# Four value blocks instead of two at the start of a decoder trunk, and a layer norm whose centering is divided between VectorE and GpSimd

## The chip, the cores and the metric

The kernel runs on one core of one Trainium2 chip. The metric is the device time of one execution in microseconds (us). The engines of the core are named as the profile names them: PE is TensorE (PEld its weight loads), DVE is VectorE, ACT is ScalarE, POOL is GpSimd, and SP issues the DMAs.

## The reference, cut to what matters

The computation is a two-layer decoder trunk on one sequence of 256 tokens with model width 2048, all in float32. Layer 0 mixes tokens with RWKV-7, layer 1 with causal differential attention. Each mixer and each gated MLP (conv-GLU) is followed by a layer norm over `ALPHA * x + h`, so there are four norms.

```python
def rwkv7_mix(x, v_first, vres, mu, w_rkv, w0, w1, w2, ...):
    xx = token_shift(x) - x
    xr, xw, xk, xv, xa, xg = (x + xx * mu[i] for i in range(6))
    r = xr @ w_rkv[0]
    k = xk @ w_rkv[1]
    v = xv @ w_rkv[2]
    w = -jax.nn.softplus(-(w0 + jnp.tanh(xw @ w1) @ w2)) - 0.5
    a = jax.nn.sigmoid(a0 + (xa @ a1) @ a2)
    g = jax.nn.sigmoid(xg @ g1) @ g2
    ...

def reference(x, ...):
    for i in range(DEPTH):
        h = rwkv7_mix(x, ...) or diff_attn_mix(x, ...)
        x = layer_norm(ALPHA * x + h, ln_g[i, 0], ln_b[i, 0])
        x = layer_norm(ALPHA * x + conv_glu(x, ...), ln_g[i, 1], ln_b[i, 1])
    return x
```

## The kernel before

**Layout.** Activations are stored transposed: 128 of the 2048 channels on the partitions, 256 tokens along the free dimension, so an activation is `KT` = 16 tiles of 128x256 ("k-tiles"). A weight matrix is read from HBM in blocks of 128 output channels; a block is 16 weight tiles of 128x128.

**Exact products.** Each float32 operand is split into a high part `hi` (a rounded copy, made by ACT) and a low part `lo` (source minus `hi`, made by DVE). A product of a block and one k-tile is hi*hi, hi*lo and lo*hi, which is three passes of 256 columns on PE. `mm3` (lines 222 to 232) issues them either as one matmul of 512 columns and one of 256 into two halves of a PSUM bank (lines 231 and 232), which `total` then adds, or "narrow" as three of 256 columns into one half (lines 227 to 229), after which one copy is enough. Weights come in DMAs of 256 KB (`raw`), and `chunk` makes `hi` (line 216, ACT) and `lo` (line 219, DVE, or GpSimd where `pool` is set). In the first stage such a chunk is four weight tiles wide (128x512).

**The first stage** is in `rwkv`. It computes the values `V` (16 blocks), three small "lora" products (one block each, `in_l`), and the first four blocks of keys and receptances (`products(0)`). That is 23 blocks, or 23 * 16 * 3 = 1104 passes of 256 columns. Every product needs its own mixture of `x` and the shifted `x`, made by `mix(i, ...)`: `xx` is the difference of neighbouring tokens (line 789), `mx` is `xx * mu + x` (line 792, DVE), and `split` writes its high part (line 196, ACT) and its low part (line 197, DVE) into `S0` or `S1`. The program text of the stage is:

1. `lead` feeds the mixture for the values tile by tile and runs the first `lg` = 2 value blocks beside it. `ramp=2` runs the first chunks of both blocks tile by tile in an order of their own (lines 243 to 258).
2. Then `_together` interleaves the loras with the other value blocks, taken in pairs into one PSUM bank (`dense_pair`).
3. Then come the mixture for the keys and `products(0)`.

**The norms.** `ln_stats` sums the channels by matmuls with a constant matrix into the PSUM tile `lnst`, whose halves are the mean and the mean square. ACT copies the mean to SBUF (`ln_dm`, line 428). DVE forms the variance (`ln_v`, line 429), ACT takes Ln and Exp (lines 434 and 435) for 1/sqrt, and DVE improves it by one Newton step (lines 436 to 438). The first value and the result both lie in the second half of `lnst`. `ln_apply` then centers all 16 tiles of `X` on GpSimd (line 450), and DVE and ACT scale and split them. At three of the four norms this runs beside the first six blocks of the next product, whose matmuls use the tiles before they are normalised (`Ahead`, lines 915 to 917). The fourth norm ends the program (`ln_finish`): there four pairs of tiles are centered by DVE, straight from the mean in PSUM, and four pairs by GpSimd.

**Order of the work.** A scheduler places the instructions of each engine by their dependences; every engine then runs its own list in order. The interleaving of streams is set by the step counts handed to `_together` and `lead`, and the number of buffers by the pools (`PACE`: `vw` are the buffers of `raw`, `hi` and `lo` in the first stage, `vp` the extra PSUM banks). All weight DMAs go through SP's queue, in order.

Of the kernel before, what the change touches and what calls it, by code (L numbers as in the profile page):

```python
# [14 lines left out]
P = 128  # L15
# [21 lines left out]
            4), lb=1, early=46.23, vw=(8, 5, 5), vp=2, ep='V', eg='A', lg=2, lr=2, la=4, ah=10, ao=12, ah0=0.05)  # L37
# [4 lines left out]
LEAD = dict(q=9, p=(), e=1, a=1, s=4, n=0.301, d=8, h=0.1, r='ACAAAAAAAAAAABBB')  # L42
FIN_P = (4, 6, 8, 10)
# [86 lines left out]
class Trunk:  # L130
# [103 lines left out]
    def dense_steps(self, src, n, xs, evac, group=1, k0=0, step=4, pool=False, narrow=False,  # L234
                    ramp=0):

        for g in range(0, len(src), group):
# [4 lines left out]
            while done < n:  # L242
                if done < ramp:

                    chunks = [(ps[j], *next(its[j])) for j in js]
                    s = chunks[0][2]
                    for i in range(s):
                        x = xs[:, k0 + done + i, :]
                        w = slice(i * P, (i + 1) * P)
                        for p, _, _, hi, lo in chunks:  # L250
                            self.nc.tensor.matmul(p[:, :T], lhsT=hi[:, w], rhs=x[:, :T], start=done + i == 0,
                                                  stop=False)
                            self.nc.tensor.matmul(p[:, T:], lhsT=lo[:, w], rhs=x[:, :T], start=False, stop=False)
                        for p, _, _, hi, lo in chunks:
                            self.nc.tensor.matmul(p[:, T:], lhsT=hi[:, w], rhs=x[:, T:], start=False, stop=False)
                        yield
                    done += s
                    continue
# [73 lines left out]
    def ln_begin(self, ahead=None, share=False):  # L332

        if self.ln_st is None:
# [4 lines left out]
            self.ln_dm, self.ln_c, self.ln_m2, self.ln_v = (  # L339
                pool.tile([P, T], F32, name=f"ln_{n}") for n in ("dm", "c", "m2", "v"))  # L340
# [79 lines left out]
    def ln_stats(self, then=None):  # L420
# [12 lines left out]
        l, rs = self.ln_m2, self.ln_rs  # L433
        nc.scalar.activation(out=l, in_=self.ln_v, func=AF.Ln)
        nc.scalar.activation(out=rs, in_=l, func=AF.Exp, scale=-0.5)
        nc.vector.tensor_tensor(out=l, in0=self.ln_v, in1=rs, op=ALU.mult)
        nc.vector.scalar_tensor_tensor(out=l, in0=l, scalar=-0.5, in1=rs, op0=ALU.mult, op1=ALU.mult)
        nc.vector.scalar_tensor_tensor(out=rs, in0=l, scalar=1.5, in1=rs, op0=ALU.add, op1=ALU.mult)

    def ln_plain(self, i, h):  # L440
        self.ln_stats()
        _all(self.ln_apply(i, h))

    def ln_apply(self, i, h):
# [7 lines left out]
        for j in range(-2, KT):  # L452
            if j < KT - 2:
                center(j + 2)
# [52 lines left out]
    def lead(self, feed, group, *args, ramp=0, ahead=4):  # L507
# [246 lines left out]
    def rwkv(self, ahead=None):  # L754
        nc, tc = self.nc, self.tc
        with ExitStack() as ctx:
# [5 lines left out]
            with ExitStack() as c1:  # L762
                gr = Groups(self, c1, S1, V, mids)
                with ExitStack() as c2:
# [6 lines left out]
                    xx = xp.tile([P, KT, T], F32, name="xx")  # L771
                    nc.gpsimd.memset(x[:, :, 0:1], 0.0)
# [6 lines left out]
                    def mix(i, dst, first=False):  # L779
                        for j in range(KT):  # L780
                            if first and j in starts:
                                load(j, starts.get(j))
                            if first and j == 0:
                                nc.sync.dma_start(out=self.par[:, :6 * KT], in_=self.a["par"][:, :6 * KT])
                            if first and j == 8:
# [720 lines left out]
```

## Time and profile before

| | |
|---|---|
| median of 3 runs | 2523.8 us (2520.84 to 2527.0) |
| the profiled execution | 2523.33 us, its span 2521.6 us |
| PE busy | 2457.5 us, 97% of the span |
| DVE busy | 2012.7 us, 80% |
| ACT busy | 1640.7 us, 65% |
| POOL busy | 165.7 us, 7% |

The profiled execution lies 0.5 us below the median. The span is the stretch the trace covers; 1.7 us of the execution lie outside it. Times below are microseconds from the start of the span. The busy share is a mean over stages: PE is at 97% over the whole but at well under half in the first 20 us.

### The profile page before, as it was taken

The numbers are of one execution on the slowest core, as the hardware profiler recorded it, in microseconds if no ns is written. First come the engines' busy times: TensorE is split into PE (matmuls) and PEld (weight loads), VectorE is DVE, ScalarE is ACT, GpSimd is POOL, SyncE is SP. The second block draws the span as 40 slices with busy tenths as digits, with TensorE's granted clock in tenths as the row PEclk, the third lists the DMA queues.
The fourth block names the chain that finished last, engine by engine and source line by source line (L and its number), as shares of the span: only waits on it lengthen the run. The fifth ranks groups of instructions, "written<-read, shape, count | busy, mean of one in ns | idle before, by whom it ended". The sixth has DMA issues, their size and how long they took to land.

```text
span 2521.6 us, 56316 instructions
## 1 busy us (share of the span) xinstructions
PE 2457.5 (97%) x18626; PEld 2166.4 (86%) x18626; DVE 2012.7 (80%) x5097; ACT 1640.7 (65%) x4237; POOL 165.7 (7%) x232
## 2 busy tenths in 40 slices
PE   7999999999999999999999999999999999999997
PEld 6997888777888888888889899988988888888886
DVE  8978888878997777776776877779987777777776
ACT  5756666545676666665666766666776666666665
POOL 1000000000300000000110200003300000000111
PEclk9999999999999999999999999999999999999998
DMA  6644443344465555666766555556465555566664
GB/s 211 199 127 108 111 107 103 106 126 126 142 200 189 190 190 190 189 190 198 215 188 188 151 167 175 169 178 184 152 200 188 188 187 189 187 188 187 189 189 139
DMA packets 276742, 428.70 MB, mean 170 GB/s; under 512 B 60632, under 2 KB 83168, under 8 KB 276448
## 3 DMA queue, kind: packets, MB, share of 16 engines
q1 hardware_dynamic: 276448, 425.10, 55.7%
q8 instruction: 146, 2.39, 0.4%
q14 instruction: 148, 1.21, 0.2%
HBM read 420.25 MB, written 6.31 MB: 169 GB/s over the span
## 4 chain that ended last, share of the span: by engine, by line
PE 81%; DVE 4%; ACT 1%; issue 1%; DMA 1%; POOL 0%; ACTq 0%; DVEq 0%; POOLq 0%
PE psd L231 43%; PE psd L232 22%; PE psd L227 2%; PE psd L228 2%; PE psd L229 2%; DVE lo L219 1%; PE psd L298 1%; PE psd L299 1%; PE psd L297 1%; DMA raw<-in_ff_up 1%; PE pss L1168 1%; PE lnst L353 0%; DVE S L197 0%; ACT hi L216 0%; PE pss L675 0%
## 5 line engine op out<-in xcount | busy, mean ns | idle before, releaser
L216 ACT CAST hi<-raw 128x256 fp32r<-128x256 f32 (+1 forms) x3036 | 1219.2, 410 | 690.5 <-PE psd L231 464.5
L219 DVE TENSOR_TENSOR lo<-raw,hi 128x256 fp32r<-128x256 f32 (+1 forms) x3034 | 1303.0, 439 | 417.2 <-ACT hi L216 373.4
L231 PE MATMUL psd<-S,hi 128*128 128x512 f32 x3000 | 1054.5, 395 | 2.6 <-DVE S L197 1.4
L232 PE MATMUL psd<-S,lo 128*128 128x256 f32 x3000 | 841.1, 280 | 3.0 <-DVE lo L219 3.0
L231 PEld LDWEIGHTS psd<-S,hi 128*128 128x128 f32 x3000 | 565.0, 188 | 133.8 <-ACT hi L216 1.7
L232 PEld LDWEIGHTS psd<-S,lo 128*128 128x128 f32 x3000 | 564.6, 188 | 5.0 <-DVE lo L219 4.7
L231 PE MATMUL psd<-hs,hi 128*128 128x512 f32 x1290 | 451.2, 394 | 0.0
L232 PE MATMUL psd<-hs,lo 128*128 128x256 f32 x1290 | 361.5, 280 | 0.0
L231 PEld LDWEIGHTS psd<-hs,hi 128*128 128x128 f32 x1290 | 241.8, 187 | 56.2 <-ACT hi L216 0.6
L232 PEld LDWEIGHTS psd<-hs,lo 128*128 128x128 f32 x1290 | 243.1, 188 | 0.3 <-DVE lo L219 0.2
L227 PE MATMUL psd<-S,hi 128*128 128x256 f32 x480 | 138.9, 289 | 2.2 <-ACT hi L216 1.9
L229 PE MATMUL psd<-S,lo 128*128 128x256 f32 x480 | 138.6, 289 | 0.7 <-DVE lo L219 0.7
L228 PE MATMUL psd<-S,hi 128*128 128x256 f32 x480 | 137.9, 287 | 0.0
L231 PE MATMUL psd<-S1r,hi 128*128 128x512 f32 x276 | 108.9, 425 | 2.3 <-ACT hi L216 1.1
L227 PEld LDWEIGHTS psd<-S,hi 128*128 128x128 f32 x480 | 90.8, 189 | 6.7 <-ACT hi L216 2.6
L229 PEld LDWEIGHTS psd<-S,lo 128*128 128x128 f32 x480 | 90.7, 189 | 5.7 <-issue 3.0
L228 PEld LDWEIGHTS psd<-S,hi 128*128 128x128 f32 x480 | 91.0, 190 | 2.0 <-issue 1.7
L227 PE MATMUL psd<-S1r,hi 128*128 128x256 f32 x284 | 85.7, 302 | 0.1
L231 PE MATMUL psd<-S1a,hi 128*128 128x512 f32 x240 | 84.6, 396 | 0.0
L371 POOL COPY ln_acc<-X 128x256 f32<-128x256 f32 x4 | 2.0, 511 | 1242.6 <-DVE X L405 1242.6
L232 PE MATMUL psd<-S1r,lo 128*128 128x256 f32 x276 | 82.0, 297 | 1.4 <-DVE lo L219 1.4
L546 DVE SCALAR_TENSOR_TENSOR gc<-gp,cpar,gc 128x256 f32<-128x256 f32 x172 | 82.2, 478 | 0.0
(304 smaller groups left out, 3541.6 us busy)
## 6 DMA issues: line engine op xcount, KB each, us to landing
raw<-in_ff_up SPq DMA_DIRECT2D x676, 256.0 KB, 3.4
raw<-in_ff_down SPq DMA_DIRECT2D x320, 256.0 KB, 2.9
raw<-in_rkv SPq DMA_DIRECT2D x192, 256.0 KB, 3.7
raw<-in_da_qk SPq DMA_DIRECT2D x122, 256.0 KB, 3.4
raw<-in_da_v SPq DMA_DIRECT2D x64, 256.0 KB, 3.0
raw<-in_da_o SPq DMA_DIRECT2D x64, 256.0 KB, 3.7
raw<-in_rw_o SPq DMA_DIRECT2D x50, 256.0 KB, 3.4
raw<-in_ff_down SPq DMA_DIRECT2D x32, 192.0 KB, 2.6
```

Source lines behind the costliest of these rows:

```text
L216: nc.scalar.copy(out=hi[:, :s * P], in_=r)
L219: eng.tensor_tensor(out=lo[:, :s * P], in0=r, in1=hi[:, :s * P].bitcast(F32), op=ALU.subtract)
L227: nc.tensor.matmul(ps[:, :T], lhsT=hi, rhs=xs[:, :T], start=first, stop=False)
L228: nc.tensor.matmul(ps[:, :T], lhsT=hi, rhs=xs[:, T:], start=False, stop=False)
L229: nc.tensor.matmul(ps[:, :T], lhsT=lo, rhs=xs[:, :T], start=False, stop=last)
L231: nc.tensor.matmul(ps, lhsT=hi, rhs=xs, start=first, stop=False)
L232: nc.tensor.matmul(ps[:, T:], lhsT=lo, rhs=xs[:, :T], start=False, stop=last)
L297: nc.tensor.matmul(o, lhsT=xh, rhs=hi, start=k == 0 and b == 0, stop=False)
L298: nc.tensor.matmul(o, lhsT=xh, rhs=lo, start=False, stop=False)
L299: nc.tensor.matmul(o, lhsT=xl, rhs=hi, start=False, stop=k == KT - 1 and b == T // P - 1)
L546: nc.vector.scalar_tensor_tensor(out=gc, in0=g[:, k:k + T], scalar=cw(k, j), in1=gc, op0=ALU.mult, op1=ALU.add)
L1168: nc.tensor.matmul(ps[:, n * P:(n + 1) * P], lhsT=KB[hr, uu, :, :], rhs=AR[hr, uu, :, :], start=True, stop=True)
```

## The change

**The lead.** `lg` becomes 4: four value blocks are run while the mixture for the values is being made, in the narrow form, four weight tiles of one block after another. `ramp` is removed with its code. The first `lo` chunk of each block is no longer made by GpSimd but by DVE like the others. The results are copied by ACT alone instead of being added by DVE. The buffers for weights grow from (8, 5, 5) to (9, 8, 8) and the extra PSUM banks from 2 to 4.

**The mixtures.** The first mixture is written as `x_shifted * mu + x * (1 - mu)`: ACT makes the second product (line 785 of the changed kernel, with `om` = 1 - mu) and DVE the rest, so `xx` isn't needed there. `xx` is formed later, in the first lora's mixture, by four DVE subtractions of 128x1024, and GpSimd makes none of it. The later mixtures are split in pairs of tiles (128x2x256).

**The norms.** Tiles 0 to 5 are centered by DVE in three pairs, right behind the variance and from the mean in PSUM; GpSimd centers the other ten. Exp writes its value to a new SBUF tile `ln_e` instead of the second half of `lnst`, and the Newton step reads it there. `ln_finish` gets the new place of Exp's value too.

```diff
-            4), lb=1, early=46.23, vw=(8, 5, 5), vp=2, ep='V', eg='A', lg=2, lr=2, la=4, ah=10, ao=12, ah0=0.05)
+            4), lb=1, early=46.23, vw=(9, 8, 8), vp=4, ep='V', eg='A', lg=4, la=4, ah=10, ao=12, ah0=0.05)
+FRONT = range(6)
...
         nc.scalar.activation(out=l, in_=self.ln_v, func=AF.Ln)
-        nc.scalar.activation(out=rs, in_=l, func=AF.Exp, scale=-0.5)
-        nc.vector.tensor_tensor(out=l, in0=self.ln_v, in1=rs, op=ALU.mult)
-        nc.vector.scalar_tensor_tensor(out=l, in0=l, scalar=-0.5, in1=rs, op0=ALU.mult, op1=ALU.mult)
-        nc.vector.scalar_tensor_tensor(out=rs, in0=l, scalar=1.5, in1=rs, op0=ALU.add, op1=ALU.mult)
+        nc.scalar.activation(out=e, in_=l, func=AF.Exp, scale=-0.5)
+        nc.vector.tensor_tensor(out=l, in0=self.ln_v, in1=e, op=ALU.mult)
+        nc.vector.scalar_tensor_tensor(out=l, in0=l, scalar=-0.5, in1=e, op0=ALU.mult, op1=ALU.mult)
+        nc.vector.scalar_tensor_tensor(out=self.ln_rs, in0=l, scalar=1.5, in1=e, op0=ALU.add, op1=ALU.mult)
...
+    def ln_center(self, tiles):
+
+        for j in tiles:
+            xs = self.X[:, j:j + 2, :]
+            self.nc.vector.tensor_tensor(out=xs, in0=xs, in1=self.ln_mean.unsqueeze(1).broadcast_to([P, 2, T]),
+                                         op=ALU.subtract)
...
-            if j < KT - 2:
+            if j < KT - 2 and j + 2 not in FRONT:
                 center(j + 2)
...
-                steps = self.dense_steps(*args, group=group, pool=True, ramp=ramp)
+                steps = self.dense_steps(*args, group=group, narrow=True)
...
+                                m = xt.tile([P, 2, T], F32, name="mp")
+                                t, m = m[:, 0], m[:, 1]
+                                nc.scalar.activation(out=t, in_=x[:, j, 1:], func=AF.Copy, scale=om[:, j:j + 1])
+                                nc.vector.scalar_tensor_tensor(out=m, in0=x[:, j, 0:T], scalar=self.p(f"mu{i}", j),
+                                                               in1=t, op0=ALU.mult, op1=ALU.add)
+                                self.split(m, dst[:, j, :])
...
-                    evv = lambda j, ps: self.total(ps, V[:, j, :])
+                    evv = lambda j, ps: nc.scalar.copy(out=V[:, j, :], in_=ps[:, :T])
...
-                t.ln_stats()
+                t.ln_stats(lambda: t.ln_center(FRONT[::2]))
```

**Where the order changes: the lead on DVE.** These are DVE's rows in the first stage after their first dozen instructions, before the change (`S_76` is `S0`, `mx` the mixture):

```order
L197 TENSOR_TENSOR S_76<-mx,S_76 128x256 x2
L792 SCALAR_TENSOR_TENSOR mx<-xx,par,xz 128x256
L197 TENSOR_TENSOR S_76<-mx,S_76 128x256
L789 TENSOR_TENSOR xx<-xz 128x256
L197 TENSOR_TENSOR S_76<-mx,S_76 128x256
L792 SCALAR_TENSOR_TENSOR mx<-xx,par,xz 128x256 x3
```

And these are DVE's first rows now (`mp` holds ACT's product and the mixture):

```order
L786 SCALAR_TENSOR_TENSOR mp<-xz,par,mp 128x256 x3
L198 TENSOR_TENSOR S_76<-mp,S_76 128x256 x3
L786 SCALAR_TENSOR_TENSOR mp<-xz,par,mp 128x256
L220 TENSOR_TENSOR lo<-raw,hi 128x512
L786 SCALAR_TENSOR_TENSOR mp<-xz,par,mp 128x256
L198 TENSOR_TENSOR S_76<-mp,S_76 128x256
L220 TENSOR_TENSOR lo<-raw,hi 128x512
```

A weight chunk's `lo` now stands in every step, beside one mixture and one split, where before two mixtures and their splits followed each other with no `lo` between them.

**Where the order changes: the first norm on DVE.** Before, from the variance on (`ln_m` is a scratch tile, `lnst` the PSUM tile):

```order
L429 SCALAR_TENSOR_TENSOR ln_v<-lnst,ln_m_9580 128x256
L219 TENSOR_TENSOR lo<-raw,hi 128x256 x2
L436 TENSOR_TENSOR ln_m_9580<-ln_v,lnst 128x256
L219 TENSOR_TENSOR lo<-raw,hi 128x256
L437 SCALAR_TENSOR_TENSOR ln_m_9580<-ln_m_9580,lnst 128x256
```

Now:

```order
L413 SCALAR_TENSOR_TENSOR ln_v<-lnst,ln_m_9488 128x256
L432 TENSOR_TENSOR X<-X,lnst 128x512 x3
L420 TENSOR_TENSOR ln_m_9488<-ln_v,ln_e 128x256
L220 TENSOR_TENSOR lo<-raw,hi 128x256
L421 SCALAR_TENSOR_TENSOR ln_m_9488<-ln_m_9488,ln_e 128x256
```

Three centerings of a pair stand where two `lo` stood, and the Newton step has two operands in SBUF instead of one in SBUF and one in PSUM. At the other two norms of this kind the rows change alike; at the fourth only the operand does.

More of the change, by code (lines that the diff above doesn't have):

```diff
@@ L242, in dense_steps @@
             while done < n:
[L243 to L258, printed above, removed]
                 for j in js:
@@ L338, in ln_begin @@
             pool = mk("lnp")
-            self.ln_dm, self.ln_c, self.ln_m2, self.ln_v = (
-                pool.tile([P, T], F32, name=f"ln_{n}") for n in ("dm", "c", "m2", "v"))
+            self.ln_dm, self.ln_c, self.ln_m2, self.ln_v, self.ln_e = (
+                pool.tile([P, T], F32, name=f"ln_{n}") for n in ("dm", "c", "m2", "v", "e"))
             self.ln_mean, self.ln_rs = self.ln_st
@@ L505, in ln_finish, with lead @@
             nc.sync.dma_start(out=out[:, j:j + 2, :], in_=xs)
-    def lead(self, feed, group, *args, ramp=0, ahead=4):
+    def lead(self, feed, group, *args, ahead=4):
         fed = 0
@@ L771, in rwkv @@
                     xx = xp.tile([P, KT, T], F32, name="xx")
+                    om = xp.tile([P, KT], F32, name="om")
                     nc.gpsimd.memset(x[:, :, 0:1], 0.0)
```

52 lines of the change are left out of this document (30 added, 22 removed).

## The prediction

> **What bounds the kernel now.** I read the page's busy shares first, then a table of stretches of the first 150 us, PE's waits there, and single rows of the timeline. The page says PE is the bound.
>
> ```profile
> PE 2457.5 (97%) x18626; PEld 2166.4 (86%) x18626; DVE 2012.7 (80%) x5097; ACT 1640.7 (65%) x4237; POOL 165.7 (7%) x232
> ```
>
> So an edit pays where PE has nothing to do or runs slowly. The stretches (columns: us, then busy us and instructions of PE, PEld, DVE, ACT, POOL, granted clock, DMA share, GB/s) show that this is the start:
>
> ```profile
> 8.00:12.00 4.00, 2.58 (x7) 1.78 (x8) 2.60 (x4) 1.02 (x2) 3.87 (x4) 1.00 1.06 350
> ...
> 16.00:20.00 4.00, 1.44 (x7) 0.95 (x5) 4.00 (x9) 2.34 (x6) 1.72 (x3) 0.97 0.55 209
> ...
> 20.00:23.00 3.00, 0.55 (x2) 0.04 (x2) 3.00 (x9) 2.83 (x7) 0.00 (x0) 0.50 0.00 0
> ...
> 60.00:148.00 88.00, 88.00 (x715) 86.61 (x714) 85.40 (x195) 64.15 (x137) 0.27 (x2) 1.00 0.59 183
> ...
> 26.00:148.50 122.50, 121.40 (x951) 117.28 (x951) 119.09 (x268) 88.40 (x191) 0.27 (x2) 1.00 0.61 190
> ```
>
> Until 23 us PE is starved while DVE is full; from 60 us PE is never idle, and DVE hardly (119.09 of 122.5 us). PE's rows show a second loss, its speed:
>
> ```profile
> 8.03 0.58 PE L251 MATMUL psd<-S,hi 128*128 128x256 f32 x1 [8.03 <-ACT hi L216]
> ...
> 22.98 0.58 PE L232 MATMUL psd<-S,lo 128*128 128x256 f32 x1 [2.45 <-DVE lo L219]
> ...
> 24.00 0.63 PE L231 MATMUL psd<-S,hi 128*128 128x512 f32 x1
> ...
> 24.64 0.63 PE L231 MATMUL psd<-S,hi 128*128 128x512 f32 x1
> ...
> 26.95 0.39 PE L231 MATMUL psd<-S,hi 128*128 128x512 f32 x1
> ...
> 27.30 0.39 PE L231 MATMUL psd<-S,hi 128*128 128x512 f32 x1
> ...
> 154.14 0.29 PE L227 MATMUL psd<-mid,l 128*128 128x256 f32 x1
> ```
>
> One k-tile of a block (three passes of 256 columns) takes 0.64 us at 24 us and 0.35 us at 27 us: 0.213 and 0.117 us a pass. The speed comes some 3.4 us after PE runs without a hole (22.98 to 26.4). The matmul at 154.14 is the first behind the stage's 1104 passes. By 32.8 us (a moment that the sum needs) these are done:
>
> ```profile
> L231 PE MATMUL psd<-S,hi 128*128 128x512 f32 x22 | 9.8, 470 | 2.6 <-DVE S L197 1.4 <-ACT hi L216 1.1
> ...
> L232 PE MATMUL psd<-S,lo 128*128 128x256 f32 x21 | 6.9, 336 | 2.5 <-DVE lo L219 2.5
> ...
> L251 PE MATMUL psd<-S,hi 128*128 128x256 f32 x8 | 3.8, 477 | 8.8 <-ACT hi L216 8.8
> ```
>
> That is 2 * 22 + 21 + 3 * 8 (lines 253 and 255 also have 8) + 2 narrow ones = 91 passes. The other 1013 take until 154.1, 0.120 us each.
>
> **The lead, part by part.** Durations of DVE and ACT come from starts that follow each other (mean spacing is shorter than duration):
>
> ```profile
> 9.74 3.00 DVE L792 SCALAR_TENSOR_TENSOR mx<-xx,par,xz 128x256 f32<-128x256 f32 x3
> ...
> 10.91 6.81 POOL L789 TENSOR_TENSOR xx<-xz 128x256 f32<-128x256 f32 x9
> ...
> 19.67 1.26 DVE L792 SCALAR_TENSOR_TENSOR mx<-xx,par,xz 128x256 f32<-128x256 f32 x3
> ...
> 29.03 1.89 DVE L219 TENSOR_TENSOR lo<-raw,hi 128x512 fp32r<-128x512 f32 x3
> ...
> 137.33 1.09 DVE L197 TENSOR_TENSOR S<-mx,S 128x256 fp32r<-128x256 f32 x3
> ...
> 147.84 0.69 DVE L219 TENSOR_TENSOR lo<-raw,hi 128x512 fp32r<-128x512 f32 x1 [0.72 <-ACT hi L216]
> ...
> 182.28 1.22 DVE L1220 TENSOR_TENSOR KB<-KB,pc 128x1024 f32<-128x1024 f32 x1
> ...
> 1273.01 0.50 ACT L895 ACTIVATE S<-X,par 128x256 fp32r<-128x256 f32 x1
> ...
> 60.07 0.71 ACT L196 CAST S1r<-mx 128x256 fp32r<-128x256 f32 x2
> ```
>
> Three mixtures take 1.26 us alone, 0.395 each, and 3.00 beside GpSimd's subtractions. A `lo` of 128x512 takes 0.60, a split of 128x256 0.335, a subtraction of 128x1024 about 1.15.
>
> *Feed.* A step of the new lead is one k-tile mixed and one weight chunk split: DVE 0.395 + 0.335 + 0.60 = 1.33 us. ACT has its product (nearest: the scaled copy at 1273.01, 0.40 to 0.50), a cast (0.31) and a `hi` (0.60 by its duration): 1.3 to 1.4. PE gets 12 passes for it: 1.41 us fast, 2.56 slow. Before, a chunk fed PE as much but there were two per four k-tiles mixed, so PE starved. On SP's queue the first weights keep their place as fifth DMA; the others move ahead among the x loads, each 256 KB for 1.33 us, with 128 KB of x: 290 GB/s, which the row at 8.00:12.00 exceeds. The x tiles are then needed later too, so I cost this at nothing; if that cover went, PE would wait for the chunk named.
>
> *PE.* It starts at 8.0 as before. It then has 12 passes every 1.33 us and needs 2.56 for them while slow, so it has no hole, and gains speed after 3.4 us or one such window more: 13 us, say. It has done 23 passes by then, and the other 169 of the four blocks (192 passes) need 19.8 us: 32.8. Against 91 passes in the trace that is 101 passes, or 101 * 0.117 = 11.8 us ahead. With the remaining 912 at 0.120 PE could be done at 142.1.
>
> *DVE then decides.* Work up to the stage's last `lo`, counted in the order of the changed kernel: 92 `lo` at 0.60 (two more than before, GpSimd's), 96 mixtures at 0.395, 40 paired splits at 0.60, 16 single ones at 0.335, four of 128x1024 at 1.15, and 9 for small things: 55.2 + 37.9 + 24.0 + 5.4 + 4.6 + 4.1 = 131.2 us. The same count for before gives 130.3. So the edits to the mixtures cancel on DVE; the gain is that DVE loses its slow stretch beside GpSimd (3.00 against 1.26) and no longer idles for x. It starts at about 4.4 (x lands at 3.0, then ACT's two steps), has 2.9 us done by 8.0, and the other 128.3 run to 136.3. With the idle of before (122.5 - 119.09 = 3.4) and 2 us for waits on ACT in the lead, since ACT is as full, the last `lo` is ready at 141.7, not 148.5 as before, and PE's last chunk behind it takes 1.4: 143.1.
>
> PE's 142.1 and DVE's 143.1 nearly coincide. Two engines that must both run without a hole lose more than either alone; I add 2 us, an estimate, and take 145.1 against 154.1: **-9.0 us**, between -11.8 (PE alone sets it) and -2 (lead fed in 1.9 us steps, below). ACT's additional products and copies fall in a stretch with 64.15 of 88 us busy, and cost nothing behind the lead. The larger pools hide SP's waits; nothing else uses that SBUF then. What follows 154 us is bound by PE and its chain, and moves ahead whole.
>
> **The three inner norms.**
>
> ```profile
> 649.63 2.09 DVE L219 TENSOR_TENSOR lo<-raw,hi 128x256 fp32r<-128x256 f32 x6
> ...
> 657.39 13.61 POOL L450 TENSOR_TENSOR X<-X,ln_dm 128x256 f32<-128x256 f32 x16 [10.82 <-ACT ln_dm L428]
> ...
> 657.82 1.48 DVE L219 TENSOR_TENSOR lo<-raw,hi 128x256 fp32r<-128x256 f32 x2
> ...
> 660.00:666.00 6.00, 6.00 (x52) 6.00 (x51) 6.00 (x12) 3.35 (x9) 6.00 (x8) 1.00 0.37 126
> ...
> 666.00:672.00 6.00, 5.44 (x39) 4.73 (x38) 6.00 (x12) 3.04 (x9) 5.00 (x6) 1.00 0.20 51
> ...
> 672.00:686.00 14.00, 13.52 (x106) 12.67 (x105) 13.26 (x40) 13.13 (x36) 0.00 (x0) 1.00 0.53 150
> ```
>
> PE loses 0.56 + 0.48 = 1.0 us here, for `lo`. Beside GpSimd's centering a `lo` takes 0.74 instead of 0.34. Six centerings fewer free DVE 5.1 us earlier (6 * 0.85), which spares some six doublings of 0.4: -2.4. Added are three centerings from PSUM (0.62 each by the rows below): +1.9, and the Newton step now reads two SBUF operands, as `lo` does: 3 * 0.3 to 0.4, +1.1. DVE ends nearly even, but the additions come first and PE's `lo` wait behind them. PE takes a `lo` (two k-tiles) every 0.71 us; counted along the new order, the fourth and fifth `lo` come 0.3 and 0.5 us after PE wants them, and from the eighth on they come early. So PE loses 0.8 instead of 1.0: I take 0. The ends are -1.0 for a norm (no wait left) and +3.0 (all additions on PE's path); the count along the order lies near the first.
>
> **The last norm** lies on the end of the program:
>
> ```profile
> 2506.69 5.51 POOL L491 TENSOR_TENSOR X<-X,ln_dm 128x256 f32<-128x256 f32 x8 [14.63 <-ACT ln_dm L428]
> ...
> 2506.99 2.47 DVE L493 TENSOR_TENSOR X<-X,lnst 128x512 f32<-128x512 f32 x4
> ...
> 2509.55 0.39 ACT L435 ACTIVATE lnst<-ln_m 128x256 f32<-128x256 f32 x1 [2.03 <-DVE X L493]
> ...
> 2509.97 0.42 DVE L436 TENSOR_TENSOR ln_m<-ln_v,lnst 128x256 f32<-128x256 f32 x1 [0.51 <-ACT lnst L435]
> ```
>
> Exp waited 2.03 us for DVE's centering, which reads the other half of the tile it writes; with `ln_e` it runs during it, and DVE is spared 0.5. But the three Newton instructions, 0.42 each with one operand in PSUM, then read SBUF twice while GpSimd works until 2512.2: + 3 * 0.4. Net **+0.7**, between -0.5 (no collision) and +1.2.
>
> By the Trainium skill, "SBUF — State Buffer", section "SBUF: two separate sides", a DVE instruction with two SBUF inputs and a GpSimd one that reads SBUF exclude each other for the whole instruction. The trace agrees in kind (0.74 against 0.34 at 657.82); if each of the three waited out a whole GpSimd addition (5.51 / 8 = 0.69), the tail would cost +1.6 and the sum 0.9 us more.
>
> **Sum.** 2523.3 - 9.0 + 0 + 0.7 = 2515.0 us. The profiled execution stands 0.5 us below the median, which I leave in the range. A change under 0.2% (5 us) can't be told from none here.
>
> **Rivals.** *PE alone sets the stage* (20%): DVE's buffers, eight instead of five, hide its unevenness, -11.8, and the norms win 1: 2511. For it speaks that PE waited for nothing from 60 to 148 us in spite of a full DVE; against it, that DVE has little spare.
>
> *The lead's feed is slower* (20%): ACT and DVE hand each k-tile to and fro four times with three buffers. At 1.9 us a step instead of 1.33 the 16 steps end 9 us later and nearly all is gone: 2522, no change.
>
> *PE stays slow, and it is slower than before* (10%): if a step takes over 2.56 us, PE has holes even at half speed and doesn't gain its speed in the lead. Four blocks would last till 8.7 + 16 * 2.6 = 50, and the 912 passes behind them 109 us: 159 against 154, so 2529. Before, holes of 1 to 2.5 us kept it slow from 8 to 26 us, which speaks for it; against it, DVE's 1.33. The Trainium skill, "TensorE: Matmul & The Clock Gate", section "A second HAM failure mode: psum-queue depth-cycling", says that short pauses between groups of matmuls send the clock back and forth; with four banks taken in turn it would give this rival's time. The trace agrees only in that half speed lasted while there were holes.
>
> **How the numbers follow.** My sum 50%, the others as given. Faster by over 0.2%: the sum and PE alone, with 2 of the 20 for the slow feed, 72%; within 0.2%: 19%; slower: 9%. The range takes in PE alone with its norms (2509) and half of the slow feed (2521).
>
> **What the profile will show.** Right: PE at 0.117 us a pass by about 13 us, no PE wait over 1 us between 13 and 33, the first matmul on `mid` of the gates near 145, then PE waits for `lo` before it that weren't there; POOL with 10 centerings of 8.5 us at a norm; Exp at 2507.5 counted from the old tail, Newton rows of 0.7 to 0.9. Wrong: a lead that ends after 37 us; PE waits of many us on `S L198`; or the stage's gain given back by 240 us, where the recurrence starts.

## The result, and the profile after

The changed kernel takes 2511.0 us (median of 12 runs, 2506.25 to 2518.66) against 2524.2 us (2518.66 to 2529.46) for the kernel before: a ratio of 0.9948, 95% interval 0.9936 to 0.9961, or 13.2 us less (9.8 to 16.2). The forecast was 2515.0 with a range of 2509 to 2521. The profiled execution took 2506.71 us, its span 2504.9; that is 4.3 us under the median of its runs, so the two traces differ by 16.7 us and not all of it is the change.

The busy shares hardly tell the two kernels apart (engines, busy us, share, instructions):

```profile
PE 2447.8 (98%) x18650; PEld 2162.3 (86%) x18650; DVE 2006.1 (80%) x5066; ACT 1641.1 (66%) x4215; POOL 138.9 (6%) x200
```

The stretches of the first stage do (columns as in the prediction):

```profile
8.00:12.00 4.00, 3.62 (x16) 3.40 (x17) 3.64 (x8) 3.85 (x10) 0.00 (x0) 1.00 1.06 373
12.00:16.00 4.00, 4.00 (x36) 4.00 (x36) 4.00 (x10) 4.00 (x11) 0.00 (x0) 1.00 1.06 375
...
20.00:23.00 3.00, 3.00 (x28) 3.00 (x28) 3.00 (x8) 3.00 (x8) 0.00 (x0) 1.00 1.05 381
...
30.00:60.00 30.00, 27.26 (x208) 25.54 (x207) 27.79 (x50) 19.15 (x37) 0.00 (x0) 1.00 0.61 194
60.00:100.00 40.00, 40.00 (x314) 38.65 (x313) 40.00 (x80) 27.35 (x52) 0.00 (x0) 1.00 0.58 183
```

Where PE had 2 matmuls between 20 and 23 us it now has 28, with DVE full in both. PE's rows give the moment at which it comes to full speed, and the stage's end:

```profile
8.38 0.58 PE L228 MATMUL psd<-S,hi 128*128 128x256 f32 x1 [8.38 <-ACT hi L217]
...
11.40 0.41 PE L228 MATMUL psd<-S,hi 128*128 128x256 f32 x1
11.62 0.36 PE L229 MATMUL psd<-S,hi 128*128 128x256 f32 x1
11.81 0.28 PE L230 MATMUL psd<-S,lo 128*128 128x256 f32 x1
11.93 0.28 PE L228 MATMUL psd<-S,hi 128*128 128x256 f32 x1
...
145.57 0.29 PE L228 MATMUL psd<-mid,l 128*128 128x256 f32 x1
```

A pass takes 0.21 us until 11.8 and 0.12 from there: PE comes to full speed 3.4 us after its first matmul, where before the change that came only at 26.4 us. The first matmul on `mid`, the end of the stage, comes at 145.57 instead of 154.14: 8.6 us earlier. By 32.8 us, the moment that the forecast counted at, 193 passes have begun, against 91 before. PE's waits from 0 to 150 us are two groups, the start and a new one, `lo`, nearly all of it between 40 and 52 us, in the first lora (line waited for: us in total, times, longest):

```profile
PE psd L228 <- ACT hi L217: 8.4, 1, 8.4
PE psd L230 <- DVE lo L220: 3.0, 5, 1.1
```

Behind the stage the distance grows. DVE's row that makes a norm's variance starts at 657.35, 1386.11, 1784.17 and 2506.65 us before, and at 645.81, 1371.93, 1768.30 and 2489.81 now: 11.5, 14.2, 15.9 and 16.8 us earlier. From the stage's end to the first variance it is 503.2 us before and 500.2 now, in code that the change does not touch; from the first variance to the fourth 1849.3 and 1844.0; from the fourth to the end of the span 14.9 and 15.1. So the traces' 16.7 us are 8.6 in the first stage, 3.0 in the recurrence, 5.3 between the norms, and 0.2 lost at the tail. Which of these the change owns is for the experiments.

### The profile page after: what moved, and what is told of

Same layout as the page of the kernel before. It is cut to its first block, busy times and chain, and to the rows that moved or that the text cites. A ratio compares the mean times of both kernels' runs of the same rounds, so it can differ in the third digit from the quotient of the medians.

```text
span 2504.9 us, 56249 instructions
## 1 busy us (share of the span) xinstructions
PE 2447.8 (98%) x18650; PEld 2162.3 (86%) x18650; DVE 2006.1 (80%) x5066; ACT 1641.1 (66%) x4215; POOL 138.9 (6%) x200
## 4 chain that ended last, share of the span: by engine, by line
PE 83%; DVE 3%; DMA 1%; ACT 1%; issue 1%; POOL 0%; SPq 0%; ACTq 0%; DVEq 0%; POOLq 0%
PE psd L232 43%; PE psd L233 22%; PE psd L228 2%; PE psd L229 2%; PE psd L230 2%; PE psd L282 1%; PE psd L283 1%; PE psd L281 1%; DVE lo L220 1%; DMA raw<-in_rw_o 1%; PE psd L924 1%; PE psd L923 1%; PE psd L925 1%; PE lnst L337 1%; PE pss L1176 1%
## 5 line engine op out<-in xcount | busy, mean ns | idle before, releaser
L232 PE MATMUL psd<-S,hi 128*128 128x512 f32 x2976 | 1043.8, 395 | 0.0
L232 PEld LDWEIGHTS psd<-S,hi 128*128 128x128 f32 x2976 | 559.6, 188 | 129.7
L228 PE MATMUL psd<-S,hi 128*128 128x256 f32 x512 | 148.4, 290 | 10.0 <-ACT hi L217 9.8
L229 PE MATMUL psd<-S,hi 128*128 128x256 f32 x512 | 147.4, 288 | 0.0
L228 PEld LDWEIGHTS psd<-S,hi 128*128 128x128 f32 x512 | 97.5, 190 | 14.5 <-ACT hi L217 10.2
L229 PEld LDWEIGHTS psd<-S,hi 128*128 128x128 f32 x512 | 97.6, 191 | 1.7 <-issue 1.5
L228 PE MATMUL psd<-S1r,hi 128*128 128x256 f32 x284 | 85.8, 302 | 1.1 <-ACT hi L217 1.1
L229 PE MATMUL psd<-S1r,hi 128*128 128x256 f32 x284 | 81.8, 288 | 0.0
```

What stands on the lines that cost most here:

```text
L228: nc.tensor.matmul(ps[:, :T], lhsT=hi, rhs=xs[:, :T], start=first, stop=False)
L229: nc.tensor.matmul(ps[:, :T], lhsT=hi, rhs=xs[:, T:], start=False, stop=False)
L232: nc.tensor.matmul(ps, lhsT=hi, rhs=xs, start=first, stop=False)
```

## The experiments

**The two halves of the change alone.** The lead alone:

```diff
-FRONT = range(6)
+FRONT = range(0)
-        l, e = self.ln_m2, self.ln_e
+        l, e = self.ln_m2, self.ln_rs
```

> The changed first stage with the norms of before: GpSimd centers all 16 tiles at the three inner norms, Exp writes into PSUM. Changed kernel 2511.0, before 2524.2. Theory A (my prediction's account: the lead carries all, the norms are even, and the remaining 4 us of the trace's shift are the draw between executions): as fast as the changed kernel or 0.7 us faster for the tail, 2510 to 2512, and at the norms the shift against before stays what it is ahead of them. Theory B (each edited norm gives about 1 us, the tail nothing): 2514 to 2516, the first stage 8.6 us shorter (first matmul on mid near 145.6 in both theories) and the shift standing at 8.6 to 10.6 from there to the end. The Newton rows at a norm should last 0.4 us, not 0.96.

The norms alone (the kernel before with `FRONT`, `ln_center` and `ln_e` put in, its first stage left as it was):

```diff
+FRONT = range(6)
...
+        nc.scalar.activation(out=e, in_=l, func=AF.Exp, scale=-0.5)
...
+        self.ln_stats(lambda: self.ln_center(FRONT[::2]))
...
```

> The first stage of before with the norms of the changed kernel (six tiles by DVE in pairs, Exp's value in SBUF). Theory A (norms even, tail between +0.2 and +0.7): 2524 to 2525, no difference from before; the first matmul on mid at 154.1 as before. Theory B (about 1 us won at each inner norm): 2521 to 2522, and against the trace of before the variances of the second, third and fourth norm come 1, 2 and 3 us earlier.

Measured: the lead alone 2510.8 us, ratio to before 0.9956 (0.9941 to 0.9972), so 11.1 us (7.1 to 14.9); the norms alone 2520.4, ratio 0.9990 (0.9977 to 1.0003), so 2.5 us less, between 5.8 less and 0.8 more. By its time the lead alone falls to theory A (2510 to 2512) and the norms alone lie beyond both, but the intervals are wider than the distance between the theories. The traces are finer. Time from variance to variance, in us:

| kernel | stage's end | to norm 1 | 1 to 2 | 2 to 3 | 3 to 4 | 1 to 4 |
|---|---|---|---|---|---|---|
| before | 154.1 | 503.2 | 728.8 | 398.1 | 722.5 | 1849.3 |
| lead alone | 145.2 | 502.0 | 728.0 | 396.2 | 722.8 | 1847.0 |
| norms alone | 154.8 | 500.4 | 726.0 | 398.0 | 721.5 | 1845.5 |
| after | 145.6 | 500.2 | 726.1 | 396.4 | 721.5 | 1844.0 |

With five more kernels that have the norms of the change (below), these take 726.0 to 726.5 from the first norm to the second and 1843.4 to 1845.5 from the first to the fourth, 1844.6 in the mean of seven; the norms of before 1848.1 in the mean of two, which differ by 2.3. The norms give some 3.5 us, 2.1 of it behind the first.

That this is won at the norms, and not somewhere in the hundreds of us behind them, is seen from the time between a variance and the start of the 401st PE matmul behind it, some 60 us later and the same matmul in every kernel. At the first norm it is 62.1 and 61.5 us with the norms of before (the kernel before and the lead alone), and 59.5 to 60.0 in the seven kernels; at the third 61.0 and 61.3 against 59.8 to 60.9; at the second 58.9 and 57.8 against 57.1 to 58.9, which cannot be told apart. So theory B is right in kind, but the first norm gives twice its 1 us, the third about 1 and the second nothing that shows.

Where this comes from is not seen in PE's busy time. These are the 28 us behind each of the three variances, before the change:

```profile
657.35:685.35 28.00, 26.96 (x210) 25.39 (x210) 27.08 (x63) 21.16 (x58) 13.61 (x16) 1.00 0.38 110
1386.11:1414.11 28.00, 25.88 (x194) 24.31 (x194) 26.00 (x60) 20.07 (x55) 13.62 (x16) 0.97 0.39 108
1784.17:1812.17 28.00, 27.23 (x214) 25.89 (x214) 27.22 (x63) 21.42 (x58) 13.62 (x16) 1.00 0.39 117
```

The same with the lead alone:

```profile
647.12:675.12 28.00, 27.40 (x216) 26.09 (x215) 26.77 (x61) 20.62 (x56) 13.62 (x16) 1.00 0.38 114
...
1771.31:1799.31 28.00, 27.31 (x215) 25.98 (x215) 27.41 (x63) 21.62 (x59) 13.61 (x16) 1.00 0.40 120
```

And after the whole change:

```profile
645.81:673.81 28.00, 26.99 (x222) 26.41 (x222) 27.50 (x69) 21.90 (x61) 8.18 (x10) 1.00 0.44 132
...
1768.30:1796.30 28.00, 27.22 (x222) 26.39 (x221) 27.27 (x68) 21.61 (x60) 8.08 (x10) 1.00 0.49 141
```

At the first norm PE is busy 27.40 us with the lead alone and 26.99 after the change, yet does 216 matmuls there and 222 here. A matmul's row lasts 0.28 us and the next starts 0.117 us behind it, so a start that comes up to 0.16 us late leaves PE "busy". At 0.117 us a pass 28 us hold 239: before the change 29 were missing at the first norm, 3.4 us, where PE's idle time and its waits both show 1.0:

```profile
PE psd L916 <- DVE lo L219: 0.7, 3, 0.3
...
PE psd L915 <- ACT hi L216: 0.3, 1, 0.3
```

After the change 17 are missing, 2.0 us. The Trainium skill, "Perfetto Trace Analysis", section "Identifying the Most-Contended Engine", warns that pipelining makes a matmul's busy time a poor measure and advises the weight loads' share; the trace agrees: PEld stands at 25.39, 26.09 and 26.41 us in the three first rows, in the order of the counts.

Stretches of 4 us show where the matmuls were missing. Before the change PE stays slow long after GpSimd has ended, at 671 us:

```profile
673.30:677.30 4.00, 3.98 (x32) 3.65 (x31) 4.00 (x13) 3.98 (x12) 0.00 (x0) 1.00 0.27 71
...
681.30:685.30 4.00, 3.82 (x29) 3.63 (x30) 4.00 (x13) 4.00 (x12) 0.00 (x0) 1.00 0.65 190
```

After the change it is slower than before between 4 and 12 us behind the variance, and full from there:

```profile
649.80:653.80 4.00, 3.56 (x28) 3.14 (x26) 4.00 (x7) 1.12 (x4) 4.00 (x6) 1.00 0.20 70
...
657.80:661.80 4.00, 4.00 (x36) 4.00 (x35) 4.00 (x13) 3.45 (x11) 0.00 (x0) 1.00 0.57 171
```

DVE is nearly full in both 28 us, and does 63 instructions before the change and 69 after. Fewer of them run beside GpSimd: the mean `lo` lasts 0.49 us instead of 0.54, the mean split of a tile 0.42 instead of 0.55. How much of the gain is this, and how much the other order, is not separated.

**Exp's tile and the front, one at a time.** The change with Exp in PSUM again:

```diff
-        l, e = self.ln_m2, self.ln_e
+        l, e = self.ln_m2, self.ln_rs
```

> The changed kernel, but Exp writes its value into the PSUM tile again and the Newton step reads it there; six tiles are still centered by VectorE. What is read is the time from one norm's variance to the next in the profile, first to second: 728.7 and 728.0 us with the norms of before, 725.9 to 726.5 in seven kernels with the changed ones; and from the first to the fourth: 1849.3 and 1847.0 against 1843.4 to 1845.5. Theory A (the gain of the norms comes from the ten centerings instead of sixteen): 726.0 to 726.8 and 1843.5 to 1846; Exp waits about 1.4 us for the third addition, and the Newton rows take 0.42 us. Rival B (it comes from Exp's own tile): 728 and 1847 or more.

And with `ln_e`, but all tiles centered by GpSimd:

```diff
-FRONT = range(6)
+FRONT = range(0)
```

> The changed kernel with all 16 tiles centered by GpSimd again and only Exp's value in its own SBUF tile. Read as for the kernel with the front alone. Theory A (Exp's tile gives nothing at an inner norm and costs the doubled Newton rows): 728.0 to 729.2 from the first norm to the second, 1847 to 1850 from the first to the fourth. Rival B: 726 to 727, 1845.

Measured (one run each, 2507.7 and 2518.2 us, which tells little): the front alone 727.0 from the first norm to the second and 1844.1 from the first to the fourth, Exp alone 729.2 and 1850.7. From the variance to the 401st matmul at the first norm it is 60.4 and 62.7 us. Theory A holds in both, though two of its four ranges are missed, by 0.2 and 0.7 us: the ten centerings carry the gain, and Exp's own tile alone gives none. Whether it adds some tenths beside the centerings stays open. Rows of ACT and DVE show what Exp's tile costs. With the front alone:

```profile
649.40 0.38 ACT L419 ACTIVATE lnst<-ln_m 128x256 f32<-128x256 f32 x1
650.27 0.41 DVE L420 TENSOR_TENSOR ln_m<-ln_v,lnst 128x256 f32<-128x256 f32 x1
...
651.15 0.41 DVE L421 SCALAR_TENSOR_TENSOR ln_m<-ln_m,lnst 128x256 f32<-128x256 f32 x1
```

With Exp's tile alone:

```profile
651.61 0.41 ACT L419 ACTIVATE ln_e<-ln_m 128x256 f32<-128x256 f32 x1
...
652.41 0.95 DVE L420 TENSOR_TENSOR ln_m<-ln_v,ln_e 128x256 f32<-128x256 f32 x1
```

Here a Newton row with one operand in PSUM takes 0.41 us beside GpSimd, and one with both in SBUF 0.95.

**How many tiles DVE should center.** Four, eight and sixteen instead of six:

```diff
-FRONT = range(6)
+FRONT = range(4)   # then range(8), and range(16)
```

> The changed kernel with four tiles centered by VectorE instead of six. Theory A (the gain grows with the tiles taken from GpSimd, 0.35 us a tile from 728.35 with none to 726.2 with six): 726.9 from the first norm to the second, 1846 from the first to the fourth. Rival B (any number above none gives the same): 726.2 and 1844.6.

> The changed kernel with eight tiles centered by VectorE instead of six. From the first norm to the second 726.2 with six and 734.0 with sixteen, where VectorE's list also changed its order ahead of the norm. Theory A (each tile moved to VectorE beyond six costs alike, 0.8 us): 727.8 and, over three norms, 1848. Rival B (the best number lies between; the cost at sixteen is that of another order): 725.5 to 726.5 and 1843 to 1846.

> The changed kernel with all 16 tiles of an inner norm centered by VectorE in eight pairs, none by GpSimd; the last norm is left as it is. In the traces so far the time from the first norm's variance to the second norm's is 728.7 and 728.0 us with the norms of before and 726.0 to 726.5 with those of the change, and PE loses its time not in waits that show but in fewer matmuls per microsecond: at full speed 36 narrow passes stand in 4 us, and in the 28 us behind the variance 36 were missing before and 17 after the change. Theory A (the loss is what stands ahead of lo on DVE plus the doubling beside GpSimd): five more pairs of 0.62 us cost 3.1, and eight lo and two Newton rows without GpSimd save 10 * 0.4 = 4.0: about even, 725 to 726.5 from norm to norm, 2509 to 2512 in all. Rival B (the doubling beside GpSimd is nearly the whole loss): 724, and 2505 to 2507. Rival C (DVE's additions ahead of lo are nearly the whole): 729, and 2517 to 2520.

Measured from the first norm to the second, and from the first to the fourth: four 728.5 and 1847.6, six 726.2 and 1844.6 (means of seven), eight 727.4 and 1846.3, sixteen 734.0 and 1863.4. With sixteen the kernel takes 2529.3 us, ratio 1.0026 (1.0016 to 1.0037), slower than before. With four and eight tiles one run took 2515.3 and 2512.6 us. Each of the other three numbers is of one profile, so what lies under 1 us is open. Both neighbours lie above all seven profiles with six, and so they do to the 401st matmul at the first norm: 62.0 us with four and 61.0 with eight, where six have 59.5 to 60.0. So the best number is likely near six. Four fits neither of its theories, for behind the first norm it gains nothing over none (728.4), which no run explains; eight lies between its two. The count of passes in the expectation for sixteen set 36 in 4 us as the full rate, which is too many: a stretch also counts the matmuls that reach into it. At 0.117 us a pass it is 34. All three of its theories were too low, and the rows show a reason that none named:

```profile
651.66 4.86 DVE L432 TENSOR_TENSOR X<-X,lnst 128x512 f32<-128x512 f32 x8
...
683.82 1.09 DVE L465 SCALAR_TENSOR_TENSOR S<-X,par,S 128x256 fp32r<-128x256 f32 x2
684.84 3.16 DVE L220 TENSOR_TENSOR lo<-raw,hi 128x256 fp32r<-128x256 f32 x8
```

PE's row at that place is the first with a `lo` of the block behind the six that run ahead of the norm:

```profile
685.31 0.58 PE L233 MATMUL psd<-S,lo 128*128 128x256 f32 x1 [4.28 <-DVE lo L220]
```

The additions put the scaling of the tiles off, the rest of it comes in one piece behind PE's last block ahead of the norm, and the next `lo` stands behind that: a wait of 4.28 us, behind which PE is also slow (granted clock 0.50 from 684 to 688). DVE's list also holds the raw tiles' splits (line 904) in other places than after the change, so the loss is not that of the five additional additions alone.

**The lead with two blocks.** How far the ends of two first stages can be told apart is seen from seven kernels whose first stage is the same, instruction by instruction: after the change, the lead alone, the front alone, Exp alone, and four, eight and sixteen tiles by DVE. It ends at 145.2 to 148.6 us, in the mean at 146.4.

```diff
-... lg=4, ...
+... lg=2, ...
-... for j in range(n, KT, 2))), 11 * 5))
+... for j in range(n, KT, 2))), 13 * 5))
```

> The changed kernel with two value blocks in the lead instead of four; the first mixture by ACT and DVE, the larger pools and all else stay. Theory A (it is the number of blocks that feeds PE): with two blocks a k-tile feeds 6 passes, so PE has holes and stays at 0.213 us a pass until the lead ends at 22 to 24 us, with 96 passes done; at 0.117 from some 26.4 us it stands at about 167 passes at 32.8 us where the changed kernel has 192 (25 passes, 3 us). The first matmul on mid comes at 148 to 149, the time is 2513 to 2515. Rival B (four blocks are the whole gain): back to 154 and 2520 or more. Rival C (the mixture's new form and GpSimd's absence are the whole gain): 145.6 and 2511, no change.

Measured: 2516.9 us, ratio 0.9975 (0.9964 to 0.9986), stage's end at 151.3. Theory A in kind, between A and B in size:

```profile
12.00:16.00 4.00, 3.90 (x31) 3.69 (x31) 4.00 (x10) 4.00 (x11) 0.00 (x0) 1.00 1.06 362
16.00:20.00 4.00, 2.98 (x20) 2.21 (x18) 4.00 (x11) 4.00 (x12) 0.00 (x0) 1.00 1.05 391
...
26.00:33.00 7.00, 4.73 (x41) 4.52 (x40) 4.98 (x10) 4.56 (x11) 0.00 (x0) 1.00 0.78 264
```

Its mechanism was wrong in one point: PE is at full speed from 12.4 us here too (passes 0.12 us apart) and is starved, not slow: 20 matmuls between 16 and 20 us, and 41 between 26 and 33, where four blocks have some 60. Of the 8.6 us between the two traces all other edits of the first stage carry 2.9 (154.1 to 151.3), the third and fourth block 5.7, each from one profile.

**The lead with the old mixture.**

```diff
-                                nc.scalar.activation(out=t, in_=x[:, j, 1:], func=AF.Copy, scale=om[:, j:j + 1])
+                                eng = nc.vector if j in (0, 4, 8, 12) else nc.gpsimd
+                                eng.tensor_tensor(out=xx[:, j, :], in0=x[:, j, 0:T], in1=x[:, j, 1:], op=ALU.subtract)
...
```

> The changed kernel with the first mixture as before: the differences made tile by tile, 4 by DVE and 12 by GpSimd, no products by ACT; the four wide differences in the first lora's mixture fall away. Theory A (DVE's work beside GpSimd is what cost): 12 of GpSimd's subtractions, 0.76 us each, stretch DVE's mixtures and lo beside them; a step of the lead takes about 1.85 us instead of 1.33, PE's lead ends 5 to 6 us later, the waits of 3.0 us for lo in the first lora go since DVE is spared 4.6 us there, and the first matmul on mid comes 2 to 4 us later, at 148 to 149: 2513 to 2515. Rival B (only the sum of DVE's own work counts, and that is less by 3 us here): first mid at 142 to 143, 2508. Rival C (holes return and keep PE slow beyond 13 us): 151 or later, 2517 or more.

Measured: 2508.7 us, ratio 0.9945 (0.9929 to 0.9960), stage's end at 146.6, between theories A and B and within the spread of the seven; neither the times nor the ends can be told apart from those of the change. PE's waits to 150 us:

```profile
PE psd L228 <- ACT hi L217: 8.5, 2, 7.6
PE psd L230 <- DVE lo L220: 1.1, 3, 0.7
PE psd L229 <- DVE S L198: 0.6, 1, 0.6
```

Two things cancel. The waits for `lo` fall from 3.0 to 1.1 us, since the four wide differences are gone. But the lead is slower: PE's passes stand 0.21 us apart until 17.4 us, where the seven kernels come to full speed at 11.0 to 14.4, and by 28 us 117 of them have begun, against 141 to 158. That is 24 to 41 passes, 2.8 to 4.8 us, somewhat less than the 5 to 6 us that theory A put there. It is not GpSimd's doing alone: until 28 us DVE's mixtures are stretched from 0.48 to 0.60 us each, but DVE also waits 3.4 us for `hi` (0.8 after the change). With four blocks the mixture's new form gives nothing measurable in the end.

**Who sets the stage's end.** Three kernels move DVE's work. First, the later mixtures read `x` for `xx`, and the wide differences are gone, so this kernel leaves out a part of the computation:

```diff
-                                    nc.vector.tensor_tensor(out=xx[:, j:j + 4, :], in0=x[:, j:j + 4, 0:T],
-                                                            in1=x[:, j:j + 4, 1:], op=ALU.subtract))
...
-                                nc.vector.scalar_tensor_tensor(out=m[:, k], in0=xx[:, j + k, :],
+                                nc.vector.scalar_tensor_tensor(out=m[:, k], in0=x[:, j + k, 0:T],
```

> The changed kernel without the four wide differences (4.6 us of DVE, between 27 and 46 us): the later mixtures read x in the place of the difference, so this kernel leaves out that part of the computation. After the change PE waits 3.0 us for lo between 40 and 52 us. Theory A (DVE's work in the first lora, not PE, sets the end of the stage): the waits go and the first matmul on mid comes at 142 to 143 instead of 145.6, where PE's 1104 passes alone put it; 2507 to 2509. Rival B (PE sets it and the waits only show where slack stood): 145 to 145.6, 2511. Rival C (DVE sets it to the end): 141, the whole 4.6 us, 2506.

Measured: 2505.2 us, ratio 0.9928 (0.9916 to 0.9941), and PE's only wait to 150 us is that at the start; the stage ends where theory C put it:

```profile
PE psd L228 <- ACT hi L217: 8.1, 1, 8.1
...
141.16 0.29 PE L228 MATMUL psd<-mid,l 128*128 128x256 f32 x1
```

That is also about PE's own limit: it has no wait left, and 1104 passes at 0.117 us from its start at 8.1 would end at 137.3, with 2.5 us more for the slow start (5.2 us at 0.21 a pass), so all its holes come to about 1.4 us. So some 141 us are what PE alone needs, and the other 4.4 us after the change (5.2 by the mean of the seven) are DVE's, but for 0.3 by which PE began earlier here.

Second, half of the first lora's mixture with ACT's product, and two of the four differences made in the second lora (the name `om1` is 1 - mu of the first lora):

```diff
+                                if i == 1 and j < 8:
...
+                                    nc.scalar.activation(out=m[:, k], in_=x[:, j + k, 1:], func=AF.Copy, scale=om1[:, j + k:j + k + 1])
...
-                            yield from mix(mi, S1, diff=i == 0)
+                            yield from mix(mi, S1, diff=((8, 12), (0, 4), ())[i])
```

> The changed kernel with the first eight tiles of the first lora's mixture made like the values' mixture (ACT the one product, DVE the rest) and two of the four wide differences made in the second lora instead of the first. DVE has 2.3 us less before 46 us and 2.3 us more between 50 and 80 us; ACT has 8 products of 0.4 us more. Theory A (only the place of DVE's work counts, since DVE ends its last lo 5 us ahead of PE): of the 3.0 us of waits in the first lora 2 go and none come back, first matmul on mid at 143 to 144, 2508.5 to 2510. Rival B (DVE full from 50 to 130 us hands the wait on): 145.6, 2511. Rival C (ACT, busy three quarters there, delays the hi): 146 or later.

Third, six blocks in the lead:

```diff
-... lg=4, ...
+... lg=6, ...
-... for j in range(n, KT, 2))), 11 * 5))
+... for j in range(n, KT, 2))), 9 * 5))
```

> The changed kernel with six value blocks in the lead instead of four. Each k-tile then feeds 18 passes, 2.1 us at full speed, for which DVE needs 0.73 + 1.5 * 0.6 = 1.63 us: DVE gains some 0.5 us a k-tile. Theory A (PE's feed decides, and DVE gets ahead): the lead's 288 passes end at 44 us, DVE is 8 us ahead for the first lora, its waits of 3.0 us go, first matmul on mid at 142 to 143, 2508. Rival B (with six blocks on eight buffers of hi and lo DVE can't run ahead, and the loras wait at the lead's end as before): 145 to 146, 2511. Rival C (six chunks for the first tiles arrive too slowly, PE has holes at half speed up to 20 us): 148 or later, 2514.

Measured: the later differences 2513.8 us, ratio 0.9961 (0.9948 to 0.9974), stage's end 149.6; six blocks 2515.2, ratio 0.9965 (0.9954 to 0.9975), stage's end 152.7. (In these two some matmuls on `mid` already run inside the stage, five from 135.2 us and two from 121.6; the end given is that of the stage's own passes.) Neither gained. The later differences fall under rival C by their number alone; so do the six blocks, but not by its mechanism, for PE has no holes up to 20 us. There PE is full until 52 us and pays later:

```profile
28.00:36.00 8.00, 8.00 (x70) 8.00 (x69) 8.00 (x16) 5.16 (x11) 0.00 (x0) 1.00 0.83 220
36.00:44.00 8.00, 8.00 (x71) 8.00 (x70) 5.64 (x11) 5.07 (x13) 0.00 (x0) 1.00 0.94 329
...
130.00:140.00 10.00, 7.16 (x55) 6.47 (x53) 10.00 (x21) 5.99 (x11) 0.00 (x0) 1.00 0.27 93
```

DVE stands idle for 2.4 us between 36 and 44, towards the end of the lead, where it waits for one cast of ACT. From 8 to 140 us DVE is busy 122.5 us here and 129.1 after the change, 6.7 less, and the stage ends 7.1 us later. 2.9 us of this are lost by 52 us, while PE has enough to do, and 4.8 between 80 and 130 us, mostly to ACT's casts again; between 52 and 80 us 1.0 is won back. That the idle time of DVE comes back as the stage's end fits these sums; no run takes it apart. For the later differences the same sum is 126.5, 2.6 us less, and the stage ends 4.0 later; there PE also began 0.5 us later, and ACT waited 13.5 us for weights instead of 7.3, so its cause is left open.

**The recurrence.** Its code is that of before in all kernels, and from the stage's end to the first variance they take 499.1 to 505.2 us. The granted clock differs too: here are the same 50 us of the two traces, before and after, which do not hold quite the same instructions, since the stage ended 8.6 us apart.

```profile
500.00:550.00 50.00, 47.76 (x691) 36.73 (x690) 34.73 (x98) 22.67 (x60) 0.27 (x2) 0.92 0.49 128
```

```profile
500.00:550.00 50.00, 48.87 (x885) 38.19 (x884) 37.39 (x105) 25.20 (x66) 0.00 (x0) 1.00 0.51 134
```

Summed over 50 stretches of it (width times what the clock is short of 1), the shortest lacks 6.9 us (499.1) and the longest 15.5 (505.2), before 10.3 (503.2) and after 8.6 (500.2). But the clock goes with the length only loosely: six kernels that lack 10.2 or 10.3 us take anything from 500.4 to 504.3. What settles the matter is the norms alone: up to the first variance PE, DVE, ACT and POOL run the same instructions in the same order as before the change, and yet the recurrence is 2.8 us shorter. So the 3.0 us between the traces need no work of the change; that it is the clock is likely, not shown.

## Why the prediction was right, and where not

The forecast's range held and faster was its likeliest case, but its likeliest sum, 8.3 us less, lies outside the measured 9.8 to 16.2: the range was wide enough to cover a term that was wrong. The terms one by one:

- **The lead: 9.0 forecast, 8.6 in the trace** (8.1 by the mean of the seven kernels and the two traces with the old stage). The first half of the working held: PE was at full speed at 11.8 us (forecast 13; 11.0 to 14.4 in the seven kernels), had begun 193 passes by 32.8 us (forecast 192; 181 to 199), and its own limit is about 141.2 (forecast 142.1), shown by the kernel without differences. The second half, "DVE then decides", is right in kind, but its numbers met by luck. The forecast has DVE's last `lo` ready at 141.7, PE 1.4 us behind it, and adds 2 us. In the trace the last `lo` ends at 138.9 and PE needs 6.7 us more:

```profile
136.40 2.50 DVE L220 TENSOR_TENSOR lo<-raw,hi 128x512 fp32r<-128x512 f32 x4
```

  The trace of before could have told it: there the last `lo` ends at 148.5 and the stage at 154.1, 5.6 us later and not 1.4. What DVE costs PE is lost earlier, most of it between 40 and 52 us at the four differences in the first lora, which the forecast did not name. So the 2 us were of a fitting size without being the loss that they stood for.
- **The rivals of the lead.** PE did not set the stage alone: 4.6 us less of DVE's work moved its end by 4.4 against the trace after the change. The feed was not 1.9 us a step. PE did not stay slow: 36 matmuls between 12 and 16 us. The rule of the Trainium skill cited for that rival, "TensorE: Matmul & The Clock Gate", section "A second HAM failure mode: psum-queue depth-cycling", speaks of pauses between groups of matmuls; with four banks in turn this lead had none from 13 to 33 us that PE's waits show, so the run does not test it.
- **The three inner norms: 0 forecast, about 3.5 us less.** This is the step that failed. "PE loses 0.56 + 0.48 = 1.0 us here" took PE's loss from its idle time, and the count of matmuls shows 3.4 us at that norm. Hence the forecast's bounds allowed a gain of 1.0 a norm at most, where the first norm gave 2.1, and the count along the order compared with the wrong sum: the waits that it foresaw, 0.8 us, are there (1.0 in the list), but they are not the loss. The move of the centerings alone gives the gain.
- **The tail: 0.7 forecast, about 0.2.** Eleven profiles with `ln_e` have 15.1 us from the fourth variance to the end, three with Exp in PSUM 14.9. DVE's and ACT's rows of the tail after the change:

```profile
2489.86 6.09 POOL L482 TENSOR_TENSOR X<-X,ln_dm 128x256 f32<-128x256 f32 x8 [14.64 <-ACT ln_dm L412]
...
2490.72 0.42 ACT L419 ACTIVATE ln_e<-ln_m 128x256 f32<-128x256 f32 x1
...
2492.54 0.42 DVE L420 TENSOR_TENSOR ln_m<-ln_v,ln_e 128x256 f32<-128x256 f32 x1
2492.99 0.83 DVE L421 SCALAR_TENSOR_TENSOR ln_m<-ln_m,ln_e 128x256 f32<-128x256 f32 x1
2493.85 0.84 DVE L422 SCALAR_TENSOR_TENSOR lnst<-ln_m,ln_e 128x256 f32<-128x256 f32 x1
2494.72 1.88 DVE L489 TENSOR_TENSOR X<-X,lnst 128x512 f32<-128x512 f32 x3
```

  Exp is early as forecast, but two Newton rows of three are stretched, by 0.41 us each, not three. Of the Trainium skill's rule, "SBUF — State Buffer", section "SBUF: two separate sides", the traces show the kind (0.41 us with an operand in PSUM, 0.83 to 0.96 in most rows with two in SBUF, though the first such row took 0.42), not the size worked out from it, a whole GpSimd addition of 0.69 us for each of three.
- **The sum.** The stage's 8.6, the norms' 3.5 and the tail's 0.2 make 11.9 us less, inside the interval of 9.8 to 16.2. The rest of the traces' 16.7 us is the recurrence, 3.0, and 1.8 between the norms, where the trace of before was slower than that of the lead alone. That the lead alone came out at 11.1 us by its median, with 9.0 in its stage, stays inside its interval (7.1 to 14.9); nothing further was found for it.

## What to carry to other kernels

Where matmuls are pipelined, count them in a stretch and multiply by their spacing: here PE's idle time and its listed waits both showed 1.0 us of a loss of 3.4. When two engines both limit a stage, look for the stretches in which the second of them is idle: with six blocks DVE did 6.7 us less by 140 us, and the stage ended 7.1 us later. Before an end is explained by one trace, see how far the same code spreads: one first stage ended at 145.2 to 148.6 us in seven kernels. An operation of VectorE beside GpSimd was cheaper here with one operand in PSUM (0.41 us against 0.95), and the division of work between VectorE and GpSimd had a best point that had to be measured, since neither none nor all was good.

## What was not expected of the hardware

The granted clock in the table of stretches reads 1.00 between 8 and 12 us, while PE's passes there stood 0.21 us apart, half of its speed: the starting speed is seen in the spacing of the rows alone. How long it lasts is not fixed either: in the seven kernels with the same first stage PE came to full speed 3.4 to 5.8 us after its first matmul (3.4 after the change, 5.8 with the lead alone). And the recurrence, whose code is the same in every kernel, took 499.1 to 505.2 us over these profiles; that spread of 6.1 us is about half of what the change won.
